# Low parts of the w3 chunks: an accumulating transfer onto a negative copy, in place of a VectorE subtraction

## The chip, the cores and the metric

The kernel runs on one core of one Trainium2 chip. The metric is the time of one execution on the device, in microseconds. The engines are called TensorE (PE), VectorE (DVE), ScalarE (ACT), GpSimd (POOL) and SyncE (SP, which issues the loads).

## What is computed

Two layers of a diffusion backbone over 256 latent tokens and 256 context tokens, in float32. Each layer is a half-step SwiGLU feed-forward sublayer (FFN), a mixer with three branches (mLSTM, a Fourier branch, a convolution), and a second FFN; each sublayer is modulated by a conditioning vector and closed by a layer norm. The change touches only the FFN:

```python
def swiglu(u, w1, w3, w2):
    return (jax.nn.silu(u @ w1) * (u @ w3)) @ w2

def ffn_sublayer(h, mod, w1, w3, w2, g, b):
    u = h * (1 + mod[1]) + mod[0]
    return layer_norm(ALPHA * h + 0.5 * mod[2] * swiglu(u, w1, w3, w2), g, b)

for l in range(DEPTH):
    x = ffn_sublayer(x, ada_x[0], ffn_w1[l, 0], ffn_w3[l, 0], ffn_w2[l, 0], ln_g[l, 0], ln_b[l, 0])
    ...
    x = ffn_sublayer(x, ada_x[2], ffn_w1[l, 1], ffn_w3[l, 1], ffn_w2[l, 1], ln_g[l, 2], ln_b[l, 2])
```

Model width is 1024 and the FFN's inner width 2816, that is 22 blocks of 128. The context runs through the same FFNs except the last.

## The kernel before, in words

Activations lie with their channels on the partitions and the tokens along the free axis: T = 512 columns where latents and context run together, T = 256 in the last FFN. Every float32 product is made from three products of fp32r operands. Both sides are split into a high part, the value rounded to fp32r, and a low part, what is left of it; `mm3` multiplies high by high (line 203), high weight by low activation (line 204) and low weight by high activation (line 205), eight times over the 1024 input channels, so one weight chunk serves 24 matmuls. `split_into` (lines 194 and 195) splits an activation into `opH` and `opL`.

Weights are streamed. `wchunk` (line 178) loads one chunk of 128x1024 float32, 512 KB, into a `raw` buffer by SP (line 186), has ScalarE write the high part `whi` (line 189) and VectorE subtract it from `raw` to the low part `wlo` (line 190). There are four raw buffers (`NR = 4`), and they are shared with `ada_job` (line 219), a background job that computes conditioning columns from `w_ada`: its loads `araw` take the same buffers, and VectorE frees them by its products (lines 236 and 238). High and low parts have five buffers each (`NW = 5`). SP issues loads in program order, and a load waits at the head of SP's queue until its buffer is free.

`gated(fts)` in `ffn` (line 445) takes blocks of the inner width: for each block `ft` it asks for a chunk of w1 and one of w3, multiplies both with the operand into the PSUM tiles `ffps`, and forms silu(first) x second. A w1 chunk and a w3 chunk so alternate. The first two w3 chunks of ffn(0, 0) and their w1 chunks are prepared ahead and kept in `ready`; every other chunk comes from line 453. The chunk work has a raised priority (`PRE = 140` places), by which the scheduler draws it forward in each engine's order. The first call takes two blocks at once and works on column halves where `ready` is empty, that is at the starts of ffn(0, 1) and ffn(1, 0); there its matmuls mix in TensorE's order with those of the sublayer before, whose `closing` (line 410) ends with a layer norm. In that norm GpSimd computes `lnrr` (line 320), a power of a 128x2 tile, once for each of the two token groups, and TensorE spreads it by `lnb` (line 332).

The sequence is ffn(0, 0), mixer(0), ffn(0, 1), ffn(1, 0), mixer(1), ffn(1, 1): about 20 to 420 us, 421 to 1159, 1159 to 1541, 1541 to 1930, 1930 to 2380 and 2381 to 2584 of the span. The last FFN has T = 256; the others have T = 512.

Of the kernel before, what the change touches and what calls it, by code (L numbers as in the profile page):

```python
# [8 lines left out]
F32 = mybir.dt.float32  # L9
F32R = mybir.dt.float32r  # L10
AF = mybir.ActivationFunctionType
ALU = mybir.AluOpType
# [3 lines left out]
P = 128  # L16
# [35 lines left out]
def hybrid_kernel(tc, x, ctx, pos, cc, wada, pcol, w1, w3, w2a, w2b, wst, wv, wg, wbr, wout, dfc, dft, idn, lnrow, out):  # L52
    nc = tc.nc
    es = ExitStack()
    cst = es.enter_context(tc.tile_pool(name="cst", bufs=1))
    wp = es.enter_context(tc.tile_pool(name="wp", bufs=4))
# [8 lines left out]
    def nm(s):  # L65
        cnt[0] += 1
        return f"{s}_{cnt[0]}"

    def slot(name, w=512, dt=F32):
        return sp.tile([P, 516], dt, tag="S", bufs=NS, name=nm(name))[:, :w]  # L70

    def pair(name, T):

        if T <= 256:
            t = slot(name, 512, F32R)
            return t[:, 0:T], t[:, 256:256 + T]
        return slot(name + "H", T, F32R), slot(name + "L", T, F32R)

    def aslot(name, w=512, dt=F32):
        return sp.tile([P, 516], dt, tag="A", bufs=NA, name=nm(name))[:, :w]  # L80
# [13 lines left out]
    def bank(pool, name):  # L94
        return pool.tile([P, 512], F32, tag="ps", name=nm(name))

    act = nc.scalar.activation
# [59 lines left out]
    def bg(n):  # L157
        if busy[0]:
            return
        busy[0] = True  # L160
        while n > 0 and queue:
            try:
                next(queue[0])
                n -= 1
            except StopIteration:
                queue.pop(0)
        busy[0] = False

    def flush():
        while queue:  # L170
            bg(1)
# [4 lines left out]
    def tick():  # L176
        debt[0] += rate[0]
        n = int(debt[0])
        debt[0] -= n
        bg(n)  # L180

    def wchunk(src, w=1024):
        tick()
        with tc.high_priority(offset=PRE):
            raw = wp.tile([P, 1024], F32, tag="raw", bufs=NR, name=nm("raw"))[:, :w]
            nc.sync.dma_start(out=raw, in_=src)
            hi = wp.tile([P, 1024], F32R, tag="hi", bufs=NW, name=nm("whi"))[:, :w]
            lo = wp.tile([P, 1024], F32R, tag="lo", bufs=NW, name=nm("wlo"))[:, :w]
            act(hi, raw, AF.Copy)  # L189
            V.tensor_tensor(lo, raw, hi.bitcast(F32), op=ALU.subtract)  # L190
        return hi, lo

    def split_into(h, l, src):
        act(h, src, AF.Copy)  # L194
        V.tensor_tensor(l, src, h.bitcast(F32), op=ALU.subtract)

    def mm3(ps, W, X, ks, cs, first=True, last=True):
        n = len(ks)
        for i, kt in enumerate(ks):
            wh = W[0][:, i * P:(i + 1) * P]  # L200
            wl = W[1][:, i * P:(i + 1) * P]
            xh, xl = X[kt][0][:, cs], X[kt][1][:, cs]
            PE.matmul(ps, wh, xh, start=first and i == 0, stop=False)  # L203
            PE.matmul(ps, wh, xl, start=False, stop=False)  # L204
            PE.matmul(ps, wl, xh, start=False, stop=last and i == n - 1)  # L205

    def proj(tiles, X, nk, T, halves):

        parts = [XR, CR] if halves and T == 512 else [slice(0, T)]
        for r in parts:  # L210
            for ps, W, *x_only in tiles:
                if r == XR or not any(x_only):
                    mm3(ps[:, r], W, X, range(nk), r)

    def streams(T):
        return [(0, XR)] if T == TX else [(0, XR), (1, CR)]
# [147 lines left out]
    def run_later():  # L364
        while later:
            later.pop(0)()
# [39 lines left out]
    def residual(ps, ys, dt, l, sub, s, r, psr):  # L406
        V.scalar_tensor_tensor(ys[dt][:, r], ps[:, psr], gatecol(l, sub, s, dt), ys[dt][:, r],
                               op0=ALU.mult, op1=ALU.add)

    def closing(ys, l, sub, T, get_chunk, X, ks, nxt):  # L410


        N = Norm()
        O = Output() if nxt is None else None
        tail = TAIL if T == 512 else 0
        U = None
        for dt in range(KT - tail):
            ps = bank(mmp, "clo")
            mm3(ps[:, 0:T], get_chunk(dt), X, ks, slice(0, T))
            for s, r in streams(T):  # L420
                residual(ps, ys, dt, l, sub, s, r, r)
                N.add(s, ys[dt][:, r], T == TX and dt == KT - 1)
            if O and dt:
                O.add(dt - 1, ys[dt - 1], col(l, C_LNG + 8 * sub + dt - 1))
        bcs = {}
        if tail:
            W = {dt: get_chunk(dt) for dt in range(KT - tail, KT)}
            for s, r in streams(T):
                for dt in range(KT - tail, KT):
                    ps = bank(mmp, "clo")  # L430
                    mm3(ps[:, 0:256], W[dt], X, ks, r)
                    residual(ps, ys, dt, l, sub, s, r, slice(0, 256))
                    N.add(s, ys[dt][:, r], s == 0 and dt == KT - 1)
                bcs[s] = N.stats(s)
        if O:
            O.add(KT - 1, ys[KT - 1], col(l, C_LNG + 8 * sub + KT - 1))
            O.finish(N)
            return None
        U = new_operand(T)
        for s, r in streams(T):  # L440
            ln_close(bcs[s] if s in bcs else N.stats(s), s, r, ys, nxt, U)
        later.append(lambda y=ys: rescale(y, l, sub))
        return U

    def ffn(l, i, X, ys, T, nxt):
        sub = 2 * i
        G = {}

        def gated(fts, halves=False):
            tiles = []  # L450
            for ft in fts:
                for n, w in enumerate((w1, w3)):
                    W = ready[ft][n] if ft in ready else wchunk(w[l, i, ft])
                    tiles.append((bank(mmp, "ffps"), W))
                ready.pop(ft, None)
            proj(tiles, X, KT, T, halves)
            for n, ft in enumerate(fts):
                p1, p3 = tiles[2 * n][0], tiles[2 * n + 1][0]
                sg = aslot("sg", T)
                act(sg, p1[:, 0:T], AF.Silu)  # L460
                V.tensor_tensor(sg, p3[:, 0:T], sg, op=ALU.mult)  # L461
                G[ft] = pair("g", T) if T == TX else (aslot("gh", T, F32R), slot("gl", T, F32R))
                split_into(G[ft][0], G[ft][1], sg)

        gated([0, 1], not ready)
        run_later()
        for ft in range(2, 7):
            gated([ft])
        for gi, grp in enumerate(GROUPS):
            def chunk(dt):  # L470
                if gi == 0:
                    return wchunk(w2a[l, i, dt], 768)
                return wchunk(w2b[l, i, gi - 1, dt])
            if gi == 2:
                flush()
                U = closing(ys, l, sub, T, chunk, G, list(grp), nxt)
                break
            for dt in range(KT):
                ps = bank(mmp, "w2ps")
                mm3(ps[:, 0:T], chunk(dt), G, list(grp), slice(0, T))  # L480
                for s, r in streams(T):
                    residual(ps, ys, dt, l, sub, s, r, r)
            for ft in grp:
                del G[ft]
            for ft in range(grp[-1] + 2, min(grp[-1] + 10, FT)):
                gated([ft])
        return U
# [443 lines left out]
    ready = {}  # L931
    for part in range(4):
# [4 lines left out]
        for kt in range(0, KT, 2):  # L937
            raw = wp.tile([P, 1024], F32, tag="raw", bufs=NR, name=nm("araw"))
            for k in range(2):
                nc.sync.dma_start(out=raw[:, 512 * k:512 * k + 512].rearrange("p (v c) -> p v c", v=2),  # L940
                                  in_=wada[0, (kt + k) * P:(kt + k + 1) * P, 0:2 * D]
# [60 lines left out]
NR = 4  # L1002
NW = 5

PRE = 140
# [123 lines left out]
```

## Time and profile before

| what | value |
|---|---|
| median of 3 runs | 2585.43 us (2583.88 to 2587.95) |
| the profiled execution | 2586.51 us |
| its span in the profile | 2584.8 us |
| mean granted clock of TensorE in it | 0.994 |
| bytes moved by queue 1 (all loads and stores of SP) | 351.54 MB |
| w1 and w3 chunks loaded | 176 of 512 KB |

The page of the profile gives busy times of each engine and groups of instructions by source line; the trace behind it gives single instructions with start and length. A releaser in brackets names what ended the idle time before an instruction. `x2` at the end of a row of SP joins two issues, and its length runs from the first to the end of the last. A matmul's length overlaps the next one's: the distance of two starts is what one takes of TensorE. The profiled execution is 1.08 us above the median.

### The profile page before, as it was taken

Reading aid. Unit: us, or ns where it says so; the run is one execution under the profiler, and the core shown is the slowest. Engines: PE = TensorE matmul, PEld = TensorE weight load, DVE = VectorE, ACT = ScalarE, POOL = GpSimd, SP = SyncE. Lnnn points to the kernel's source line nnn. Section 1 sums busy time; section 2 is a strip of 40 time slices with the busy share of each in tenths; the row PEclk is TensorE's granted clock in tenths of the full one; section 3 lists DMA queues with packets and bytes.
Section 4 is the critical chain, followed back from the end, with each engine's and each line's share of the span. In section 5 each row is a group of like instructions: output and inputs, shape, how many; then the busy total and the mean of one; then the engine's idle time right before and its main releaser. Section 6 shows DMA issues by size and latency. Waiting matters only on the chain.

```text
span 2584.8 us, 36771 instructions
## 1 busy us (share of the span) xinstructions
PE 2534.4 (98%) x14354; PEld 2156.9 (83%) x14354; DVE 1789.7 (69%) x3227; ACT 961.9 (37%) x1554; POOL 48.8 (2%) x123
## 2 busy tenths in 40 slices
PE   7999999999999999999999999999999999999998
PEld 4777779788878888888778788877788889999998
DVE  4796776988877765367655467645568888976655
ACT  4222235333432334245222234222235445455543
POOL 0000000010100000000000000000000000000000
PEclk9999999999999999999999999999999999999999
DMA  8565653222223223335544325545523335465663
GB/s 272 177 214 171 184 166 108 88 79 88 64 92 100 78 86 123 91 113 157 162 140 144 124 73 164 177 140 158 158 90 98 119 108 156 151 201 160 188 188 123
DMA packets 130030, 353.89 MB, mean 137 GB/s; under 512 B 12736, under 2 KB 27328, under 8 KB 129856
## 3 DMA queue, kind: packets, MB, share of 16 engines
q1 hardware_dynamic: 129856, 351.54, 43.9%
q8 instruction: 113, 1.85, 0.3%
q14 instruction: 61, 0.50, 0.1%
HBM read 344.12 MB, written 7.34 MB: 136 GB/s over the span
## 4 chain that ended last, share of the span: by engine, by line
PE 86%; DVE 9%; DMA 2%; issue 2%; ACT 1%; POOL 1%; SPq 0%; DVEq 0%; POOLq 0%; ACTq 0%
PE ffps L203 11%; PE ffps L205 11%; PE ffps L204 11%; PE w2ps L203 4%; PE w2ps L204 4%; PE w2ps L205 4%; PE clo L203 3%; PE clo L204 3%; PE clo L205 3%; PE br L203 2%; PE br L204 2%; PE br L205 2%; PE mg L203 2%; PE mg L205 2%; PE mg L204 2%; DVE wlo L190 2%
## 5 line engine op out<-in xcount | busy, mean ns | idle before, releaser
L189 ACT ACTIVATE whi<-raw 128x1024 fp32r<-128x1024 f32 (+1 forms) x498 | 520.5, 1047 | 1199.5 <-issue 272.3
L190 DVE TENSOR_TENSOR wlo<-raw,whi 128x1024 fp32r<-128x1024 f32 (+1 forms) x498 | 599.9, 1206 | 342.5 <-ACT whi L189 337.0
L203 PE MATMUL ffps<-opH,whi 128*128 128x512 f32 (+1 forms) x1120 | 427.7, 385 | 1.8 <-ACT opH L194 1.7
L205 PE MATMUL ffps<-opH,wlo 128*128 128x512 f32 (+1 forms) x1120 | 428.2, 384 | 0.2 <-DVE wlo L190 0.2
L204 PE MATMUL ffps<-opL,whi 128*128 128x512 f32 (+1 forms) x1120 | 426.8, 383 | 0.0
L499 DVE SCALAR_TENSOR_TENSOR cy<-cz,dww,cy 128x482 f32<-128x482 f32 (+29 forms) x480 | 289.0, 602 | 18.1 <-ACT cy L587 11.1
L238 DVE SCALAR_TENSOR_TENSOR acc<-araw,sc,acc 128x512 f32<-128x512 f32 x392 | 273.8, 747 | 27.9 <-DMA araw<-in_wada_dram 26.9
L203 PEld LDWEIGHTS ffps<-opH,whi 128*128 128x128 f32 x1120 | 209.4, 188 | 50.2 <-issue 5.5
L205 PEld LDWEIGHTS ffps<-opH,wlo 128*128 128x128 f32 x1120 | 210.2, 188 | 44.9 <-issue 1.8
L204 PEld LDWEIGHTS ffps<-opL,whi 128*128 128x128 f32 x1120 | 210.4, 188 | 44.2 <-issue 1.2
L461 DVE TENSOR_TENSOR sg<-ffps,sg 128x512 f32<-128x512 f32 (+1 forms) x88 | 54.7, 623 | 116.1 <-PE ffps L205 116.0
L203 PE MATMUL w2ps<-gh,whi 128*128 128x512 f32 x336 | 133.3, 397 | 0.0
L204 PE MATMUL w2ps<-gl,whi 128*128 128x512 f32 x336 | 132.8, 395 | 0.0
L205 PE MATMUL w2ps<-gh,wlo 128*128 128x512 f32 x336 | 132.7, 395 | 0.0
L203 PE MATMUL mg<-opH,whi 128*128 128x512 f32 (+1 forms) x384 | 130.0, 339 | 0.0
L205 PE MATMUL mg<-opH,wlo 128*128 128x512 f32 (+1 forms) x384 | 130.0, 339 | 0.0
L204 PE MATMUL mg<-opL,whi 128*128 128x512 f32 (+1 forms) x384 | 129.8, 338 | 0.0
L203 PE MATMUL qk<-opH,whi 128*128 128x512 f32 (+1 forms) x296 | 102.8, 348 | 0.0
L203 PE MATMUL ffps<-op,whi 128*128 128x256 f32 x352 | 98.9, 285 | 3.2 <-ACT op L194 3.2
L204 PE MATMUL qk<-opL,whi 128*128 128x512 f32 (+1 forms) x296 | 101.7, 344 | 0.0
L205 PE MATMUL qk<-opH,wlo 128*128 128x512 f32 (+1 forms) x296 | 101.4, 343 | 0.0
L204 PE MATMUL ffps<-op,whi 128*128 128x256 f32 x352 | 99.6, 285 | 0.0
(309 smaller groups left out, 5264.8 us busy)
## 6 DMA issues: line engine op xcount, KB each, us to landing
raw<-in_w_dram SPq DMA_DIRECT2D x176, 512.0 KB, 3.6
raw<-in_wst_dram SPq DMA_DIRECT2D x144, 512.0 KB, 3.5
araw<-in_wada_dram SPq DMA_DIRECT2D x128, 512.0 KB, 4.0
raw<-in_w2b_dram SPq DMA_DIRECT2D x64, 512.0 KB, 3.6
raw<-in_wbr_dram SPq DMA_DIRECT2D x48, 512.0 KB, 3.6
raw<-in_w2a_dram SPq DMA_DIRECT2D x32, 384.0 KB, 3.3
araw<-in_wada_dram SPq DMA_DIRECT2D x32, 256.0 KB, 4.9
raw<-in_wv_dram SPq DMA_DIRECT2D x16, 512.0 KB, 3.6
```

The costliest lines, as they stand in the source:

```text
L189: act(hi, raw, AF.Copy)
L190: V.tensor_tensor(lo, raw, hi.bitcast(F32), op=ALU.subtract)
L203: PE.matmul(ps, wh, xh, start=first and i == 0, stop=False)
L204: PE.matmul(ps, wh, xl, start=False, stop=False)
L205: PE.matmul(ps, wl, xh, start=False, stop=last and i == n - 1)
L238: V.scalar_tensor_tensor(accs[s], w, c, accs[s], op0=ALU.mult, op1=ALU.add)
L461: V.tensor_tensor(sg, p3[:, 0:T], sg, op=ALU.mult)
L499: V.scalar_tensor_tensor(dv[:, :, a:b], sv[:, :, a + o:b + o], wcols[:, j:j + 1], dv[:, :, a:b], op0=ALU.mult, op1=ALU.add)
```

## The change

A second chunk function, `wchunk_dma`, stands beside `wchunk`. It loads `raw` as before (its load is line 198 of the changed kernel, its high part line 201), has ScalarE write the negative of the high part into the low part's buffer (line 202), and lets GpSimd issue a transfer of `raw` onto that buffer that adds instead of overwriting (line 203). The low part is then raw minus high, as before. `gated` uses it for w3 wherever `ready` has no chunk: 20 chunks in ffn(0, 0) and 22 in each of the other three FFNs, 86 in all. `mm3` and the loads of w1 and w2 are untouched; the lines behind move down by 13.

```diff
+    def wchunk_dma(src):
+
+        tick()
+        with tc.high_priority(offset=PRE):
+            raw = wp.tile([P, 1024], F32, tag="raw", bufs=NR, name=nm("raw"))
+            nc.sync.dma_start(out=raw, in_=src)
+            hi = wp.tile([P, 1024], F32R, tag="hi", bufs=NW, name=nm("whi"))
+            lo = wp.tile([P, 1024], F32R, tag="lo", bufs=NW, name=nm("wlo"))
+            act(hi, raw, AF.Copy)
+            act(lo, hi.bitcast(F32), AF.Copy, scale=-1.0)
+            nc.gpsimd.dma_start(out=lo.bitcast(F32), in_=raw, accum_op=ALU.add)
+        return hi, lo
...
-                    W = ready[ft][n] if ft in ready else wchunk(w[l, i, ft])
+                    W = ready[ft][n] if ft in ready else (wchunk_dma if n else wchunk)(w[l, i, ft])
```

The program has 86 instructions fewer on VectorE, 86 more on ScalarE and 86 more on GpSimd; SP and TensorE keep their numbers. Three places show how the order moves. They all lie at the start of ffn(0, 1), where `raw_1556` is the chunk of w3[0], `raw_1561` of w1[1] and `raw_1565` of w3[1]; `whi` and `wlo` of each have the next numbers.

ScalarE at the closing of mixer(0), first before: `sq` belongs to the norm, `lnbc` is its result copied out of PSUM.

```order
644 L303 ACTIVATE sq_1493_9285<-y_1448_8997 128x256
645 L293 ACTIVATE sq_1495_9315<-y_1451_9003 128x256
646 L189 ACTIVATE whi_1557_9616<-raw_1556_9614 128x1024
647 L303 ACTIVATE sq_1503_9367<-y_1442_8985 128x256
648 L334 ACTIVATE lnbc_1501_9339<-lnb_1500_9334 128x512
```

And in the change, the same place:

```order
664 L316 ACTIVATE sq_1493_9305<-y_1448_9017 128x256
665 L306 ACTIVATE sq_1495_9335<-y_1451_9023 128x256
666 L201 ACTIVATE whi_1557_9636<-raw_1556_9634 128x1024
667 L316 ACTIVATE sq_1503_9387<-y_1442_9005 128x256
668 L202 ACTIVATE wlo_1558_9637<-whi_1557_9636 128x1024
669 L347 ACTIVATE lnbc_1501_9359<-lnb_1500_9354 128x512
```

The negative copy comes right behind the high part, with one `sq` between them, and ahead of `lnbc`.

GpSimd over the same closing, first before: it had only the powers of the norms here.

```order
66 L320 TENSOR_TENSOR lnrr_1305_8179<-lnred_1304_8176,mhalf_86 128x2
67 L320 TENSOR_TENSOR lnrr_1311_8199<-lnred_1310_8196,mhalf_86 128x2
68 L320 TENSOR_TENSOR lnrr_1499_9331<-lnred_1498_9328,mhalf_86 128x2
69 L320 TENSOR_TENSOR lnrr_1513_9471<-lnred_1512_9468,mhalf_86 128x2
70 L320 TENSOR_TENSOR lnrr_1973_12348<-lnred_1972_12345,mhalf_86 128x2
```

And in the change, the same place:

```order
86 L333 TENSOR_TENSOR lnrr_1305_8199<-lnred_1304_8196,mhalf_86 128x2
87 L333 TENSOR_TENSOR lnrr_1311_8219<-lnred_1310_8216,mhalf_86 128x2
88 L333 TENSOR_TENSOR lnrr_1499_9351<-lnred_1498_9348,mhalf_86 128x2
89 L203 DMA wlo_1558_9637<-raw_1556_9634 128x1024
90 L333 TENSOR_TENSOR lnrr_1513_9491<-lnred_1512_9488,mhalf_86 128x2
91 L203 DMA wlo_1567_9658<-raw_1565_9655 128x1024
92 L203 DMA wlo_1585_9908<-raw_1583_9905 128x1024
```

The transfer of w3[0] stands between the two powers of that closing, and that of w3[1] right behind the second.

TensorE where w3[1] is first read (`ffps_1568` is its product), first before:

```order
5093 L203 MATMUL ffps_1568_9640<-opH_1516_9481,whi_1566_9636 128x256
5094 L204 MATMUL ffps_1568_9640<-opL_1517_9482,whi_1566_9636 128x256
5095 L203 MATMUL ffps_1554_9607<-opH_1524_9489,whi_1552_9603 128x256
5096 L203 MATMUL ffps_1559_9620<-opH_1524_9489,whi_1557_9616 128x256
5097 L203 MATMUL ffps_1564_9633<-opH_1524_9489,whi_1562_9629 128x256
5098 L205 MATMUL ffps_1568_9640<-opH_1516_9481,wlo_1567_9637 128x256
5099 L203 MATMUL ffps_1568_9640<-opH_1518_9483,whi_1566_9636 128x256
```

And in the change, the same place:

```order
5142 L217 MATMUL ffps_1559_9641<-opL_1519_9504,whi_1557_9636 128x256
5143 L216 MATMUL ffps_1554_9627<-opH_1520_9505,whi_1552_9623 128x256
5144 L218 MATMUL ffps_1559_9641<-opH_1518_9503,wlo_1558_9637 128x256
5145 L218 MATMUL ffps_1568_9662<-opH_1516_9501,wlo_1567_9658 128x256
5146 L216 MATMUL ffps_1568_9662<-opH_1518_9503,whi_1566_9657 128x256
5147 L217 MATMUL ffps_1568_9662<-opL_1519_9504,whi_1566_9657 128x256
```

The low part `wlo_1567` is first read at row 5145 instead of row 5098: 47 matmuls of the other three chunks now stand ahead of it. At the start of ffn(1, 0) the same row moves from 6910 to 6957.

## Rows read from the trace of the kernel before

**Rows 1.** The page, part 1: busy us (share of the span) xinstructions
```profile
PE 2534.4 (98%) x14354; PEld 2156.9 (83%) x14354; DVE 1789.7 (69%) x3227; ACT 961.9 (37%) x1554; POOL 48.8 (2%) x123
```

**Rows 2.** Busy time by window: window, length, PE, PEld, DVE, ACT, POOL, clock, DMA share, GB/s
```profile
20.00:100.00 80.00, 76.96 (x467) 52.57 (x467) 54.18 (x110) 36.03 (x65) 0.00 (x0) 1.00 0.75 239
...
1165.00:1528.00 363.00, 363.00 (x1804) 296.38 (x1803) 221.84 (x353) 111.65 (x161) 0.00 (x0) 1.00 0.45 139
1560.00:1910.00 350.00, 349.24 (x1647) 280.40 (x1646) 191.59 (x285) 99.62 (x136) 0.00 (x0) 1.00 0.50 155
2381.00:2550.00 169.00, 168.46 (x1401) 168.46 (x1402) 99.87 (x137) 83.33 (x126) 0.00 (x0) 0.98 0.57 177
```

**Rows 3.** Groups by line and shape: count | busy us, mean ns | idle before, releaser
```profile
L190 DVE TENSOR_TENSOR wlo<-raw,whi 128x1024 fp32r<-128x1024 f32 x466 | 569.3, 1223 | 324.6 <-ACT whi L189 319.1
L189 ACT ACTIVATE whi<-raw 128x1024 fp32r<-128x1024 f32 x466 | 493.4, 1060 | 1101.9 <-issue 247.4 <-PE ffps L204 143.2 <-DMA raw<-in_w_dram 127.8
...
L205 PE MATMUL ffps<-opH,wlo 128*128 128x512 f32 x992 | 393.6, 397 | 0.2 <-DVE wlo L190 0.2
```

**Rows 4.** Timeline, start of ffn(0, 1): start us, length us, engine, line, operation
```profile
1149.53 1.06 ACT L189 ACTIVATE whi<-raw 128x1024 fp32r<-128x1024 f32 x1 [3.53 <-PE clo L204]
...
1151.97 1.22 DVE L190 TENSOR_TENSOR wlo<-raw,whi 128x1024 fp32r<-128x1024 f32 x1
...
1153.25 6.48 SPq L186 DMA_DIRECT2D raw<-in_w_dram  x2
...
1158.16 1.21 DVE L190 TENSOR_TENSOR wlo<-raw,whi 128x1024 fp32r<-128x1024 f32 x1
...
1163.63 0.71 POOL L320 TENSOR_TENSOR lnrr<-lnred,mhalf 128x2 f32<-128x2 f32 x1 [13.11 <-DVE lnred L318]
...
1163.93 1.04 ACT L189 ACTIVATE whi<-raw 128x1024 fp32r<-128x1024 f32 x1
...
1165.80 1.22 DVE L190 TENSOR_TENSOR wlo<-raw,whi 128x1024 fp32r<-128x1024 f32 x1
...
1167.07 0.39 PE L205 MATMUL ffps<-opH,wlo 128*128 128x256 f32 x1
```

**Rows 5.** Timeline of ffn(0, 0), the first w3 chunk made in the stream
```profile
55.97 1.06 ACT L189 ACTIVATE whi<-raw 128x1024 fp32r<-128x1024 f32 x1 [0.91 <-PE ffps L204]
...
57.11 1.22 DVE L190 TENSOR_TENSOR wlo<-raw,whi 128x1024 fp32r<-128x1024 f32 x1
...
63.66 0.39 PE L204 MATMUL ffps<-opL,whi 128*128 128x512 f32 x1
...
63.89 0.39 PE L205 MATMUL ffps<-opH,wlo 128*128 128x512 f32 x1
```

**Rows 6.** Transfers: queue with share of 16 engines; issues with KB, us to landing
```profile
q1 hardware_dynamic: 129856, 351.54, 43.9%
...
raw<-in_w_dram SPq DMA_DIRECT2D x176, 512.0 KB, 3.6
...
cn<-cs SPq DMA_DIRECT2D x8, 256.0 KB, 5.1
...
op<-mid SPq DMA_DIRECT2D x8, 1.0 KB, 1.7
```

**Rows 7.** Timeline, start of ffn(1, 0)
```profile
1547.97 1.22 DVE L190 TENSOR_TENSOR wlo<-raw,whi 128x1024 fp32r<-128x1024 f32 x1
...
1549.25 0.39 PE L205 MATMUL ffps<-opH,wlo 128*128 128x256 f32 x1
```

**Rows 8.** Timeline of ffn(1, 1): one w3 chunk, high part and first reading of its low part
```profile
2472.29 1.06 ACT L189 ACTIVATE whi<-raw 128x1024 fp32r<-128x1024 f32 x1 [1.48 <-issue]
...
2483.78 0.28 PE L205 MATMUL ffps<-op,wlo 128*128 128x256 f32 x1
```

## The prediction

> **What bounds the kernel now.** First I read the busy shares [rows 1]: TensorE is busy 98% of the span, VectorE 69%, ScalarE 37%. So VectorE time that is saved is worth only what TensorE waits for VectorE. Next the same by stage [rows 2]: in stretches of the four FFNs TensorE is busy 76.96 of 80, 363.00 of 363, 349.24 of 350 and 168.46 of 169 us. All its idle time there is 3.04 + 0.76 + 0.54 = 4.34 us, which caps what a lighter VectorE can give in them. Then the groups by line [rows 3]: one low part of 128x1024 costs VectorE 1223 ns, one high part costs ScalarE 1060 ns, and the 992 matmuls that read a low part over 512 columns waited for it 0.2 us in all. The subtraction that goes is nearly free today, because its results stand ready before they are read; what counts is how much later the new ones come.
>
> **The change, part by part.** 86 of the 88 w3 chunks move (two are made ahead and keep the subtraction). VectorE loses 86 x 1.223 = 105 us, all beside TensorE's work. ScalarE gains 86 negative copies of the same shape as the high part, 86 x 1.06 = 91 us, which takes it from 37% to about 41%; its idle time covers that. If it did not, the next operand of TensorE would be late, by 1.06 us. SP's loads keep their number and order. GpSimd gains 86 transfers, each of which waits for its negative copy at the head of GpSimd's queue. At two closings one stands ahead of the second lnrr, which TensorE needs: but that negative copy ends near 1152 and the lnrr starts at 1163.63 [rows 4], so this costs nothing unless one issue takes over 11 us.
>
> The term that decides is the delay **D**, from the end of the negative copy to the landing of the accumulation. The low part is now ready 1.06 + D after the high part; with the subtraction it was 1.3 (57.11 + 1.22 against 55.97 + 1.06 in [rows 5]). A raw buffer is held as much longer, and SP, which waits for a free one, issues the next load later. No accumulating transfer and none issued by GpSimd is in this trace, so D is bounded by [rows 6]. From below: a 1 KB copy lands in 1.7 us. A plain load of 512 KB takes 3.6 us, about 1.9 us above the small one. The accumulation writes 512 KB but reads two sources of that size; at the pace of the load that is 1.7 + 2 x 1.9 = 5.5 us. Issue by GpSimd, nothing at the least and about 0.7 us by its lnrr row [rows 4], brings it to some 6. From above: 256 KB (cn) has a median of 5.1 us, with 1.9 us more for twice the bytes that is 7, and beside loads I let it go to 8. **I take D = 6**, nearest to the load row with a second read, and keep 2 to 8 for the range.
>
> Where is D seen? *Start of ffn(0,1) and of ffn(1,0).* There ada loads hold three raw buffers, and w3[0], w1[1] and w3[1] go one after another through the fourth. Before [rows 4]: w3[0]'s high part starts at 1149.53, its low part ends at 1151.97 + 1.22 = 1153.19 and the next load is issued at 1153.25; that load's low part ends at 1158.16 + 1.21 = 1159.37, and the next issue follows (the same row, two issues, ends at 1153.25 + 6.48 = 1159.73); w3[1]'s high part starts at 1163.93, its low part ends at 1167.02, and TensorE reads it at 1167.07: no reserve at all. After: the negative copy ends at 1149.53 + 2 x 1.06 = 1151.7; w1[1]'s load is issued at 1151.7 + D; its low part is ready 6.1 later (1159.37 − 1153.25), at 1157.8 + D; w3[1]'s high part starts 4.5 after that (1163.93 − 1159.4) and its negative is there 2.1 later; so its low part is ready at 1164.4 + 2D. In the new order TensorE reads it 47 instructions later (row 5145, not 5098). A matmul of 512 columns starts 0.23 us after the one before ([rows 5], 63.66 and 63.89), so one of 256 takes about 0.116, and 47 take 5.5 us: the reading is due at 1172.5. The stall is 2D − 8.1, from D = 4 on: 3.9 us at D = 6. The start of ffn(1,0) shows the same pattern, with a low part that ends at 1547.97 + 1.22 = 1549.19 and is read at 1549.25 [rows 7]. Two starts: **+8 us**.
>
> *ffn(0,0).* The first chunk of this kind has its high part done at 57.03 and its low part read at 63.89 [rows 5]: 6.86 us against 1.06 + 6 = 7.06, 0.2 us short. Behind it each of 20 chunks holds its buffer 5.8 us longer, a quarter of that for each of the four buffers, against a gated tile that takes TensorE 48 x 0.23 = 11 us; the reserve grows more slowly. I put **+2.5 us** at D = 6 and, as the shortfall of 2 us at D = 8 returns in the first few tiles, 8 to 15 there.
>
> *ffn(1,1).* At 256 columns a chunk takes 24 x 0.116 = 2.8 us. From the high part's end at 2472.29 + 1.06 = 2473.35 to the first reading of the low part at 2483.78 are 10.4 us [rows 8], so 1.06 + 6 fits with 3.3 us left. The transfer engines are at 0.57 there [rows 2]. All traffic of queue 1, 351.54 MB, took 43.9% of 16 engines [rows 6] over 2584.8 us, which is 1.69 us of all engines for a load of 512 KB. Two loads and one accumulation with two reads are 4 x 1.69 = 6.8 us against 5.6 us of TensorE for the same two chunks if the second read is charged in full, and 5.1 us if it is not. Only 22 chunks meet this and loads run ahead: **+1 us**, up to 20 at worst (22 x (6.8 − 5.6) = 26 less the reserve).
>
> *Relief of VectorE.* At most the 4.34 us above; I take **−1 us**.
>
> Sum: 8 + 2.5 + 1 − 1 = +10.5 us. The profiled execution took 2586.51 us (span 2584.8 plus 1.71), 1.08 above the median of the three runs: 2597 by its own time, **2596** by the median.
>
> **The rivals.**
> *Hidden.* With D at 4 or less the term 2D − 8.1 is zero, the first chunk's 6.86 us suffice, and the time stays at 2583 to 2588. For it: the load row is 3.6 us with other traffic beside it. Against it: a second source is read, and GpSimd issues. The Trainium skill, page "Collectives: The Full Stack", section "The bandwidth ceiling: the fold count and why AG ≠ RS ≠ AR", says that an add inside a transfer reads two sources and so runs at half rate; by its 31 GB/s for one engine, two reads of 512 KB on 16 engines are an estimated 2.1 us, which gives D near 4 and a sum near zero. No row here shows such an add.
> *Transfers become the bound.* At D = 8 the two starts give 16 us, ffn(0,0) 8 to 15 and ffn(1,1) 5 to 20: 2585 + 29 to 51, so 2614 to 2636, and more beyond. For it: engines 0.75 and 0.57 busy in two of these stages [rows 2]. Against: no compact transfer in [rows 6] is above 5.1 us.
> *GpSimd waits for VectorE.* If GpSimd cannot prepare its transfer while a long VectorE row runs, an issue waits up to the 1.2 us of such a row and D is about 7: the two starts give 12 us, ffn(0,0) 5, ffn(1,1) 2, relief −1, +18 in all, 2603. For it: VectorE is busy 55 to 68% of these stages [rows 2]. Against: GpSimd's lnrr takes 0.71 us beside a busy VectorE [rows 4]. The Trainium skill, page "SBUF — State Buffer", section "Who interferes with whom", states such a lock between VectorE's two-port operations and GpSimd; no run here shows it on a transfer.
> *Faster.* The 105 us matter: ada products, whose VectorE work releases raw buffers, come earlier, the idle time of ffn(0,0) goes (3.04 us of the first 80), and the closings, where VectorE normalises, shorten. It decides from a D under 3.6 on, where the accumulation is no longer than a load. Price: up to −4.3 us in the FFNs and as much in the closings, 2577 to 2581.
>
> **How the numbers follow.** 0.2% (5.2 us) is about what a measurement of this kernel can tell from no change. Likeliest, D between 4.5 and 7: 0.38, of it 0.02 within 0.2%; hidden 0.27; transfers bound 0.18; GpSimd waits 0.10; faster 0.07. So faster 0.07, within 0.2% 0.29, slower 0.64. The range leaves out most of the faster case and the far part of the bound one: 2582 to 2636.
>
> **What would show it.** Right: VectorE near 1685 us, ScalarE near 1053; 86 accumulations that land 5 to 7 us after their issue; TensorE waits for a w3 low part at two places, about 4 us each near 1172 and 1556, and hardly elsewhere. Wrong: no such waits (D under 4), or waits at every w3 chunk of ffn(1,1) with transfer engines near 0.9, or a GpSimd queue that delays the lnrr.

## The result and the profile after

The changed kernel takes 2629.53 us (median of 4 runs, 2627.59 to 2634.86), against 2585.27 us for the kernel before on the same chip: a ratio of 1.0172, 95% interval 1.0161 to 1.0184, or 44 us slower. The forecast had been 2596 us, 11 us slower: the right sign, inside the range, and a loss of a quarter of what came. The profiled execution has a span of 2626.3 us, 41.5 us longer than before.

The page of the profile after, its busy shares [rows 1] and its queues (packets, MB, share of 16 engines; q0 is the queue of the accumulations):

```profile
PE 2545.9 (97%) x14354; PEld 2163.7 (82%) x14354; DVE 1689.1 (64%) x3141; ACT 1044.5 (40%) x1640; POOL 123.8 (5%) x209
...
q1 hardware_dynamic: 129856, 351.54, 42.5%
q0 software_dynamic: 12384, 45.09, 9.4%
...
L203 POOL DMA_DIRECT2D wlo<-raw x86 | 74.6, 868 | 1179.2 <-ACT wlo L202 826.0
...
raw<-in_w_dram SPq DMA_DIRECT2D x176, 512.0 KB, 4.3
...
wlo<-raw POOLq DMA_DIRECT2D x86, 512.0 KB, 5.7
```

VectorE is 100.6 us lighter and ScalarE 82.6 us heavier, near the 105 and 91 of the forecast. An accumulation lands 5.7 us after its issue (median), and GpSimd spends 868 ns on an issue. A load of w1 or w3 now takes 4.3 us where it took 3.6 [rows 6]. TensorE is busy 11.5 us longer although it does the same work, and idle 30 us longer (2626.3 − 2545.9 against 2584.8 − 2534.4).

What TensorE waited for (the waits of PE: us in total, times, longest):

```profile
PE adat L261 <- ACT adar L259: 23.3, 7, 6.3
PE ffps L218 <- DMA wlo<-raw: 7.5, 7, 2.6
```

In the kernel before, the first of these was a single wait of 1.6 us and the second did not exist. `adat` is TensorE's transpose of the `ada` rows, `adar` the ScalarE copy of them out of PSUM. The largest of the seven waits, in the timelines of PE, ACT, SP and POOL:

```profile
96.90 0.39 PE L218 MATMUL ffps<-opH,wlo 128*128 128x512 f32 x1
103.56 0.48 PE L261 MATMUL adat<-ident,adar 128*128 128x128 f32 x1 [6.28 <-ACT adar L259]
...
100.83 1.06 ACT L201 ACTIVATE whi<-raw 128x1024 fp32r<-128x1024 f32 x1 [7.13 <-DMA raw<-in_w_dram]
101.79 0.61 ACT L207 ACTIVATE gh<-sg 128x512 fp32r<-128x512 f32 x1
102.31 1.04 ACT L202 ACTIVATE wlo<-whi 128x1024 fp32r<-128x1024 f32 x1
103.25 0.26 ACT L259 ACTIVATE adar<-adaps 128x128 f32<-128x128 f32 x1
...
88.27 0.38 SPq L241 DMA_DIRECT2D araw<-in_wada_dram  x1
97.21 0.33 SPq L198 DMA_DIRECT2D raw<-in_w_dram  x1
...
88.50 0.86 POOL L203 DMA_DIRECT2D wlo<-raw  x1 [5.48 <-ACT wlo L202]
```

What SP waited for between 88 and 98 us, a single long wait:

```profile
SPq L198 <- DMA wlo<-raw: 8.5, 1, 8.5
```

Read from the POOL row upwards: an accumulation is issued at 88.50, beside a weight load and two ada loads that SP had issued just before, and lands after 8.7 us. SP issues nothing from 88.27 to 97.21, because the next load (the chunk of w3 that comes next) is for the raw buffer that this accumulation reads. So that w3 chunk comes late, ScalarE waits 7.13 us for it, and `adar`, which has long been possible, stands behind its high part and its negative in ScalarE's order. TensorE stands still for 6.28 us at a transpose that has nothing to do with w3. SP as a whole waited 433 us at accumulations (the waits of SP in the kernel after):

```profile
SPq L186 <- DMA wlo<-raw: 234.0, 43, 19.4
SPq L241 <- DMA wlo<-raw: 104.0, 23, 10.2
SPq L198 <- DMA wlo<-raw: 94.8, 19, 10.3
```

Such a wait is not a loss by itself, for SP runs ahead. In the kernel before it waited 1491.9 us at the subtractions:

```profile
SPq L186 <- DVE wlo L190: 1284.3, 329, 20.2
SPq L228 <- DVE wlo L190: 207.6, 76, 6.5
```

It becomes a loss where the load that is held back is needed before it lands, as above.

Behind this wait TensorE also runs slower for a while (busy time by window, columns as in [rows 2]):

```profile
97.00:103.50 6.50, 0.29 (x2) 0.00 (x0) 1.08 (x3) 2.67 (x4) 0.00 (x0) 0.69 0.51 161
103.50:105.00 1.50, 1.44 (x4) 1.25 (x5) 1.50 (x5) 0.01 (x1) 0.86 (x1) 0.50 0.41 29
105.00:107.00 2.00, 2.00 (x7) 1.57 (x7) 2.00 (x5) 0.00 (x0) 0.00 (x0) 0.68 0.82 214
107.00:109.00 2.00, 2.00 (x10) 1.59 (x10) 0.98 (x2) 1.04 (x2) 0.00 (x0) 1.00 1.06 211
```

The granted clock is 0.50 after the wait (the lower of the two levels, 1.2 GHz) and 1.00 again from 107 on. That fits the 11.5 us of extra busy time: TensorE does the same 14354 matmuls at a mean granted clock of 0.989 instead of 0.994.

**Where the time went.** Two matmuls that occur in every kernel serve as marks: the first `pS` of mixer(0) that waits, behind ffn(0,0), and a `br` in mixer(1), behind ffn(0,1) and ffn(1,0). Before, and then after:

```profile
697.52 0.67 PE L648 MATMUL pS<-qk,qk 128*128 128x256 f32 x2 [1.16 <-DVE qk L499]
2162.69 0.39 PE L204 MATMUL br<-op,whi 128*128 128x256 f32 x1 [1.15 <-DVE op L195]
```

```profile
723.60 0.67 PE L661 MATMUL pS<-qk,qk 128*128 128x256 f32 x2 [1.19 <-DVE qk L512]
2199.66 0.39 PE L217 MATMUL br<-op,whi 128*128 128x256 f32 x1 [1.17 <-DVE op L208]
```

26.1 us are lost by the first mark, 10.9 between the marks, and 4.5 from the second to the end of the span. For each run the same three differences against the kernel before, in us, with its median time and its ratio to runs of the kernel before on the same chip. The differences come from one profiled execution of each; the executions of one kernel lie up to 10 us apart (e9: 2598.6 to 2608.4), so a few us between two rows say little.

| run | to mark 1 (ffn(0,0)) | mark 1 to 2 (ffn(0,1), ffn(1,0)) | mark 2 to end (ffn(1,1)) | median us | ratio (95%) |
|---|---|---|---|---|---|
| the change | 26.1 | 10.9 | 4.5 | 2629.5 | 1.0172 (1.0161 to 1.0184) |
| e1 adar on VectorE | 29.2 | 5.1 | 4.4 | 2625.1 | 1.0150 (1.0135 to 1.0165) |
| e2 five raw, four hi/lo | 32.5 | 10.7 | 13.9 | 2640.9 | 1.0215 (1.0199 to 1.0230) |
| e8 the same, kernel before | 7.0 | 4.9 | 0.6 | 2599.4 | 1.0055 (1.0038 to 1.0071) |
| e3 VectorE adds | 1.8 | 1.5 | 0.5 | 2590.1 | 1.0014 (1.0005 to 1.0024) |
| e4 source in memory | 21.6 | 1.0 | 7.2 | 2613.7 | 1.0104 (1.0087 to 1.0121) |
| e5 hold, four copies | 32.0 | 15.0 | 53.4 | 2683.4 | 1.0376 (1.0359 to 1.0394) |
| e9 hold, two copies | 15.1 | −1.3 | 0.7 | 2601.2 | 1.0067 (1.0052 to 1.0083) |
| e6 traffic | 29.5 | 1.2 | 4.2 | 2622.9 | 1.0145 (1.0130 to 1.0160) |
| e10 half the traffic | 14.0 | 1.2 | 0.3 | 2598.9 | 1.0052 (1.0035 to 1.0069) |
| e11 plain copy | 3.9 | 2.8 | 0.9 | 2594.1 | 1.0034 (1.0021 to 1.0047) |
| e12 hold and traffic | 45.5 | 18.5 | 37.3 | 2682.7 | 1.0380 (1.0364 to 1.0395) |
| e7 not in ffn(0,0) | 4.3 | 6.3 | 3.2 | 2601.9 | 1.0061 (1.0046 to 1.0076) |
| e13 VectorE's load back | 36.8 | 10.6 | 4.6 | 2638.1 | 1.0204 (1.0187 to 1.0221) |

Mark 1 in the five runs on which the account of ffn(0,0) rests, e3, e9, e6, e12 and e13 in this order:

```profile
699.34 0.67 PE L661 MATMUL pS<-qk,qk 128*128 128x256 f32 x2 [1.16 <-DVE qk L512]
712.61 0.67 PE L665 MATMUL pS<-qk,qk 128*128 128x256 f32 x2 [1.16 <-DVE qk L516]
727.01 0.67 PE L664 MATMUL pS<-qk,qk 128*128 128x256 f32 x2 [1.16 <-DVE qk L515]
743.01 0.67 PE L664 MATMUL pS<-qk,qk 128*128 128x256 f32 x2 [1.14 <-DVE qk L515]
734.30 0.67 PE L665 MATMUL pS<-qk,qk 128*128 128x256 f32 x2 [1.17 <-DVE qk L516]
```

### The profile page after: what moved, and what is told of

It reads as the page before. It is cut to its first block, busy times and chain, and to the rows that moved or that the text cites. A ratio compares the mean times of both kernels' runs of the same rounds, so it can differ in the third digit from the quotient of the medians.

```text
span 2626.3 us, 36984 instructions
## 1 busy us (share of the span) xinstructions
PE 2545.9 (97%) x14354; PEld 2163.7 (82%) x14354; DVE 1689.1 (64%) x3141; ACT 1044.5 (40%) x1640; POOL 123.8 (5%) x209
## 3 DMA queue, kind: packets, MB, share of 16 engines
q1 hardware_dynamic: 129856, 351.54, 42.5%
q0 software_dynamic: 12384, 45.09, 9.4%
## 4 chain that ended last, share of the span: by engine, by line
PE 69%; DMA 11%; DVE 10%; issue 5%; ACT 3%; POOL 1%; SPq 0%; POOLq 0%; DVEq 0%; ACTq 0%
PE ffps L216 7%; PE ffps L218 7%; PE ffps L217 7%; DMA raw<-in_w_dram 6%; DMA wlo<-raw 4%; DVE wlo L190 3%; PE w2ps L216 2%; PE w2ps L217 2%; PE w2ps L218 2%; PE clo L216 2%; PE clo L217 2%; PE clo L218 2%; DVE cy L512 2%; PE br L217 2%; PE br L216 2%
## 5 line engine op out<-in xcount | busy, mean ns | idle before, releaser
L189 ACT ACTIVATE whi<-raw 128x1024 fp32r<-128x1024 f32 (+1 forms) x412 | 429.6, 1044 | 936.6 <-PE ffps L217 128.4
L190 DVE TENSOR_TENSOR wlo<-raw,whi 128x1024 fp32r<-128x1024 f32 (+1 forms) x412 | 494.9, 1202 | 303.9 <-ACT whi L189 300.0
L201 ACT ACTIVATE whi<-raw 128x1024 fp32r<-128x1024 f32 x86 | 91.1, 1059 | 236.0 <-DMA raw<-in_w_dram 114.9
L203 POOL DMA_DIRECT2D wlo<-raw x86 | 74.6, 868 | 1179.2 <-ACT wlo L202 826.0
L218 PE MATMUL ffps<-op,wlo 128*128 128x256 f32 x352 | 100.1, 286 | 2.9 <-DMA wlo<-raw 2.9
L216 PE MATMUL ffps<-op,whi 128*128 128x256 f32 x352 | 99.5, 287 | 3.3 <-ACT op L207 3.3
```

Source lines behind the costliest of these rows:

```text
L203: nc.gpsimd.dma_start(out=lo.bitcast(F32), in_=raw, accum_op=ALU.add)
```

## The experiments

**First theory: the queue.** The trace after suggests that the loss is `adar` behind a late chunk in ScalarE's order (theory Q), against late low parts (L), shared transfer engines (C) and ScalarE's extra copies (S). Four runs were made on it. All diffs are against the changed kernel unless another is named.

*e1: adar on VectorE.*

```diff
-            act(rows, ps[:, 0:P], AF.Copy)
+            V.tensor_copy(rows, ps[:, 0:P])
```

> The changed kernel, with one edit: the copy of the ada rows out of PSUM (adar) is made by VectorE instead of ScalarE. Theory Q (queue): the accumulation holds a raw buffer some 5 us longer, SP issues the next load late, ScalarE's high part of that chunk waits for it, and adar stands behind that high part in ScalarE's order, so TensorE's transpose adat waits 23 us in seven places and runs at half clock for some us after each. Then adat's waits fall from 23.3 us to under 6, and the time from 2629.5 to about 2598 to 2608. Theory L (late low parts): TensorE waits for the accumulated low parts themselves; then nothing changes, 2625 to 2632. Theory C (transfer engines full): the loads stay late, the wait moves to another tile, 2620 to 2632.

Measured: 2625.1 us, some 4 us better, and none of it in ffn(0,0). That is far from theory Q's 2598 to 2608, and inside what both L and C gave. The waits went elsewhere, as the timeline of PE shows:

```profile
225.05 0.47 PE L261 MATMUL adat<-ident,adar 128*128 128x128 f32 x1 [5.25 <-DVE adar L259]
342.36 0.80 PE L218 MATMUL ffps<-opH,wlo 128*128 128x512 f32 x1 [5.38 <-DMA wlo<-raw]
393.48 0.71 PE L218 MATMUL ffps<-opH,wlo 128*128 128x512 f32 x1 [2.82 <-DMA wlo<-raw]
```

So ScalarE's order is where the lateness surfaces first, not where it comes from: with that way closed, the same chunks are late at VectorE, or at the low part itself. Theory Q falls, as far as it put the cause into ScalarE's order.

*e2: five raw buffers and four pairs of high and low parts.*

```diff
-NR = 4
-NW = 5
+NR = 5
+NW = 4
```

> The changed kernel with five raw buffers instead of four, and four buffers of high and low parts instead of five (there is no more memory). Theory Q: a fifth buffer gives SP the lead back that the longer hold took; adat's waits go to under 8 us, 2590 to 2605 (a little of it lost again by the fourth pair of high and low buffers). Theory L: later landing counts for the same, and four pairs give it less lead: 2630 or more. Theory C: loads are slow because the engines are shared; one buffer more changes little, 2615 to 2630.

Measured: 2640.9 us, in the range of theory L. The control e8, the kernel before with the same numbers, lost 7.0 us to mark 1, so 25.5 of e2's 32.5 belong to the change there, as many as with four buffers (26.1), if the two losses simply add.

> The kernel before with five raw buffers and four buffers of high and low parts: the control for the run of the changed kernel with the same numbers (2641). If the fourth pair is what cost there, ffn(1,0) loses some 20 us here too, 2600 to 2610, and the fifth raw buffer bought ffn(0,0) nothing in the changed kernel. If this stays at 2583 to 2590, the loss belongs to the accumulations with less lead.

Measured for e8: 2599.4 us. Four pairs instead of five have a price of their own (14 us over the whole kernel), and it is spread over the stages. One raw buffer more does not make up for it, and does not repair ffn(0,0); five of both was not tried. In ffn(1,1) e2 lost 13.9 us where e8 lost 0.6 and the change 4.5: with four pairs TensorE waits 10.0 us for low parts there, so late low parts do cost where few buffers hold them.

*e3: the negative copy stays, VectorE adds.*

```diff
-            nc.gpsimd.dma_start(out=lo.bitcast(F32), in_=raw, accum_op=ALU.add)
+            V.tensor_tensor(lo, raw, lo.bitcast(F32), op=ALU.add)
```

> ScalarE still makes the negative copy of all 86 chunks, but VectorE adds raw to it instead of the transfer, so no accumulating transfer is left. Theory Q: the raw buffer is held only 1.06 us longer than in the kernel before; 2586 to 2592. Rival S (ScalarE's 91 us of negative copies delay what stands behind them on ScalarE): 2605 or more, with adat's waits above 10 us.

Measured: 2590.1 us. ScalarE's 86 copies and the slightly longer hold cost 1.4 in a thousand, 4 us; rival S falls. e3 is the base for the runs that follow.

*e4: the accumulation reads w3 again from memory.* The low part is also written as fp32r here instead of as float32.

```diff
-            nc.gpsimd.dma_start(out=lo.bitcast(F32), in_=raw, accum_op=ALU.add)
+            nc.gpsimd.dma_start(out=lo, in_=src, accum_op=ALU.add)
```

> The changed kernel, with the accumulation reading w3 again from memory (HBM) instead of the raw buffer. The raw buffer is free after the high part, earlier than in the kernel before; the low part still lands D after the negative copy, and the engines carry 45 MB more of reads from memory. Theory Q: adat's waits fall under 6 us, and the starts of ffn(0,1) and ffn(1,0) lose their chain through the buffer: 2583 to 2595. Theory C: the same load on the transfer engines, so 2620 or more. Theory L: the low parts are as late as before, 2620 or more.

Measured: 2613.7 us, between the theories. With the raw buffer free early, the stretch of ffn(0,1) and ffn(1,0) lost 1.0 us instead of 10.9: there the loss needs the held buffer. ffn(0,0) still lost 21.6. Something beside the raw buffer costs there: the traffic, or the low parts, which come later than in the change (7.3 us from issue to landing).

**Second theory: hold and traffic.** A transfer by GpSimd does three things: it keeps the raw buffer (theory H), it moves bytes through the engines that bring the loads (theory T), and its result is late. The next runs take them one at a time, on top of e3.

*e5 and e9: hold alone.* VectorE makes the low part; GpSimd copies 8 columns of the raw buffer to a scratch tile, four times (e5) or twice (e9).

```diff
+            V.tensor_tensor(lo, raw, lo.bitcast(F32), op=ALU.add)
+            for _ in range(4):
+                nc.gpsimd.dma_start(out=hs8, in_=raw[:, 0:8])
```

> As in the run with negative copies and a VectorE addition (2590), and in addition each of the 86 raw buffers is kept for some 8 us after its load has landed: GpSimd copies 8 columns of it to a scratch tile four times, one after another. No low part is later, and the transfer engines carry next to nothing more. Theory H (the buffer that is held longer starves the ring of loads in ffn(0,0)): 2605 to 2620, the loss in ffn(0,0). Theory T (the accumulations' own traffic slows the loads beside them, which arrive in bursts there): 2588 to 2596.

Measured: 2683.4 us. Four copies keep a buffer 14.1 us after its load has landed in ffn(0,0) (mean of 20), while the changed kernel keeps it 8.3: too large a dose, and at T = 256 far too large (53.4 us lost there). So two copies:

> The run with buffers held and no traffic, with two small copies instead of four. Four kept a raw buffer 14.1 us in ffn(0,0) after its load had landed, the changed kernel keeps it 8.4 us; two should keep it about 7 us. If the hold alone, at the changed kernel's own length, explains ffn(0,0), that stage loses 12 us or more (total 2605 or more). If it only did so at twice the length, the stage loses under 5 us: 2590 to 2597.

Measured: 2601.2 us; the hold came out at 5.8 us, somewhat shorter than in the changed kernel, and ffn(0,0) lost 15.1 us, 13.3 more than e3. Hold alone does harm there, with next to no traffic (0.72 MB on GpSimd's queue against 45.09). Between the marks it cost nothing at this length (−1.3).

*e6, e10, e11: traffic alone.* VectorE makes the low part; GpSimd accumulates the high part onto a scratch tile in memory, in full (e6), half of its columns (e10), or copies it without adding (e11).

```diff
+            V.tensor_tensor(lo, raw, lo.bitcast(F32), op=ALU.add)
+            nc.gpsimd.dma_start(out=dscr, in_=hi.bitcast(F32), accum_op=ALU.add)
```

> As in the run with negative copies and a VectorE addition (2590), and in addition GpSimd accumulates each of the 86 high parts onto a scratch tile in memory (HBM) that nobody reads: the traffic of 86 accumulations of 512 KB, without a raw buffer held and without a late low part. Theory H: 2588 to 2596. Theory T: 2605 to 2625, the loss in ffn(0,0), where the engines are busiest.

> The run with traffic only, with 512 of the 1024 columns accumulated: half the bytes, 86 transfers. Theory T with a threshold (loads are late only where a burst fills the engines): ffn(0,0) loses 3 to 10 us instead of 27, 2594 to 2602. If each transfer costs by being issued and not by its bytes, the loss stays above 20 us.

> The run with traffic only, with a plain copy of the same 512 KB instead of an accumulation, so one source is read and not two. If the second read is what makes the accumulation heavy, its time on the engines falls from 10.4% of the span toward 6%, it lands about 4 us after issue instead of 6.1, and ffn(0,0) loses 8 to 16 us instead of 27: 2598 to 2608. If not, 2615 to 2625.

Measured: 2622.9, 2598.9 and 2594.1 us. ffn(0,0) lost 27.7, 12.2 and 2.1 us more than e3. The queues and issues of e6 and of e11:

```profile
q0 software_dynamic: 12384, 45.09, 10.4%
...
dscr<-whi POOLq DMA_DIRECT2D x86, 512.0 KB, 6.1
```

```profile
q0 software_dynamic: 12384, 45.09, 4.7%
...
dscr<-whi POOLq DMA_DIRECT2D x86, 512.0 KB, 3.9
```

The same bytes and packets take 2.2 times as long on the engines when they are added, and land 2.2 us later. A plain copy of 512 KB for every w3 chunk nearly fits beside the loads; the addition does not. With half the bytes the loss is nearly half, between the two cases that the expectation named. In these runs the transfer keeps a buffer of the high parts; in e6 ScalarE waited for that three times, 10.3 us in all, each time in ffn(1,1) and never in ffn(0,0).

*e12: hold and traffic, low parts on time.* As e6, but from `raw`.

```diff
+            V.tensor_tensor(lo, raw, lo.bitcast(F32), op=ALU.add)
+            nc.gpsimd.dma_start(out=dscr, in_=raw, accum_op=ALU.add)
```

> Buffers held and traffic together, but no low part late: the accumulation reads raw, as in the changed kernel, and goes to a scratch tile in memory, while VectorE makes the low part by an addition. If hold and traffic are the cause and the late low part is not, ffn(0,0) loses 22 to 32 us, and the starts of ffn(0,1) and ffn(1,0) lose what the chain through one buffer costs there: 2618 to 2632. If the late low parts matter, under 2610.

Measured: 2682.7 us, far more than expected. To mark 1 it lost 43.7 us over e3, about hold plus traffic (13.3 + 27.7 = 41.0), so a low part need not be late at all. The buffer was kept 6.9 us there, less than in the changed kernel. Between the marks hold and traffic together cost 18.5 us, where e9 and e6 alone cost −1.3 and 1.2. The 37.3 us at the end belong at least in part to the scratch tile, which the changed kernel does not have: in ffn(1,1) GpSimd waited 16 times for the transfer before, 118.4 us in all, and the transfers landed in 8.1 us (median), while TensorE takes about 5.6 us for two chunks by the prediction's working. In e6 the same waits (15, 97.2 us) held no raw buffer, and cost 4.2.

*e7: ffn(0,0) left as it was.*

```diff
-(wchunk_dma if n else wchunk)(w[l, i, ft])
+(wchunk_dma if n and (l, i) != (0, 0) else wchunk)(w[l, i, ft])
```

> The changed kernel, but ffn(0,0) keeps the VectorE subtraction: 66 of 86 chunks moved. All theories that put most of the loss into ffn(0,0) expect the loss of that stage, some 25 us, to go: 2600 to 2608. If the stages are not independent (a delay in ffn(0,0) hides one later), 2608 to 2620.

Measured: 2601.9 us. 21.8 of the 26.1 us to mark 1 go, and the other stages do not get worse (6.3 and 3.2 us instead of 10.9 and 4.5); all in all 27.7 us hang on 20 of the 86 chunks.

*e13: VectorE's load put back.* Alone, the two causes add up to 41 us in ffn(0,0), but the changed kernel loses only 24.3 over e3.

```diff
             nc.gpsimd.dma_start(out=lo.bitcast(F32), in_=raw, accum_op=ALU.add)
+            for c in (0, 512):
+                V.tensor_tensor(vs, raw[:, c:c + 512], hi[:, c:c + 512].bitcast(F32), op=ALU.subtract)
```

> The changed kernel, with VectorE's load put back: for each of the 86 chunks VectorE makes the subtraction into a scratch tile that nobody reads (two halves of 512 columns). Buffers, transfers and low parts are as in the changed kernel. Hold alone cost ffn(0,0) 13.5 us and traffic alone 27.3, together 43.0, but the changed kernel loses 24.5 there. If the lighter VectorE is what gives some 16 us back (it frees the ada buffers earlier), ffn(0,0) now loses 35 to 43 us and the time is 2638 to 2655. If the scratch tile in memory made the traffic of those runs dearer than the changed kernel's own, ffn(0,0) stays at 22 to 28 us and the time at 2628 to 2634.

For the four losses that the expectation names the table has 13.3, 27.7, 43.7 (e12) and 24.3 us, all over e3. Measured: 2638.1 us, 36.8 us to mark 1, 10.7 more than the changed kernel (8.6 more by the two median times). The lighter VectorE thus gives back about 10 us there. That it does so by freeing the ada buffers earlier fits SP's waits for VectorE's ada products in this stage (40 to 420 us of the span), 98.8 us in the changed kernel and 111.9 here, but was not tested by itself. The rest of the gap (41 against 35) may be the dearer scratch transfers, 10.4% against 9.4% of the span; that was not separated.

No run beats the kernel before.

## Why the prediction was wrong in size

**Right.** VectorE came to 1689.1 us (about 1685 forecast) and ScalarE to 1044.5 (1053). The deciding quantity was right: D was put at 6 us; the negative copy of the timeline above ends at 102.31 + 1.04 = 103.35, GpSimd issues at 103.64, and the median from issue to landing is 5.7, together 6.0. GpSimd did not wait for VectorE: each of the 86 issues follows the end of its negative copy by 0.3 us (once 1.0) and takes 868 ns, 1031 at most. So the rival "GpSimd waits for VectorE", which named the Trainium skill, page "SBUF — State Buffer", section "Who interferes with whom", shows nothing here. TensorE's waits for `lnrr` also stayed as they were, 6.5 us in 11 times.

**Near in number, only partly for the reason given.** The starts of ffn(0,1) and ffn(1,0) were put at 8 us. Between the marks 10.9 were lost, and 1.0 when the accumulation does not hold the buffer (e4). The chain through the fourth buffer runs as forecast, and TensorE waits for w3[1]'s low part at both starts, but only 1.19 and 1.23 us: D was 4.9 to 5.0 us for w3[0] and w3[1] of both stages, for which 2D − 8.1 is under 2. Of the rest, 6.4 us are waits of `adat` (1.97, 2.64 and 1.79 us), which the prediction did not have, and the second of them lies at 1334.7, far behind the start; behind that one the clock also falls to 0.50. That 8 comes near 10.9 is in part luck.

**The term that failed: ffn(0,0), +2.5 us; it cost 26.1** (24.3 over e3). The step was "each of 20 chunks holds its buffer 5.8 us longer, a quarter of that for each of the four buffers, ...; the reserve grows more slowly". Three things were wrong in it. It weighed the hold against the reserve of the w3 low parts alone, though the buffers are shared with the ada loads, SP issues in order, and any load behind a held buffer is late, whoever needs it. What TensorE waited for was mostly not a low part but `adat`, whose `adar` stands behind a late w3 chunk in ScalarE's order: 16.9 us of `adat` against 2.2 us of low parts in this stage. The hold alone makes 13.3 us (e9, at 5.8 us of hold). It charged the traffic to ffn(1,1) alone. There it cost little; ffn(0,0), where weight and ada loads together fill the engines to 0.61 and 0.63 already, went to 0.68 and 0.76, and its traffic alone makes 27.7 us (e6). The rows of before and of after, by window:

```profile
60.00:160.00 100.00, 98.37 (x488) 76.82 (x487) 82.72 (x134) 26.31 (x37) 0.00 (x0) 1.00 0.61 189
160.00:240.00 80.00, 80.00 (x385) 63.33 (x384) 64.41 (x100) 25.34 (x33) 0.00 (x0) 1.00 0.63 193
```

```profile
60.00:160.00 100.00, 92.39 (x446) 72.58 (x445) 70.47 (x117) 28.87 (x38) 3.45 (x4) 0.97 0.68 197
160.00:240.00 80.00, 74.70 (x362) 57.78 (x360) 50.62 (x85) 27.94 (x35) 6.03 (x7) 0.96 0.76 212
```

A mean of 0.76 hides the bursts: the accumulation issued at 88.50 has three loads beside it and lands after 8.7 us. And no term allowed for the clock: TensorE's busy time grew by 11.5 us over the whole kernel.

**ffn(1,1), +1 us; it cost 4.5**: one wait of 2.58 us for a low part at 2438.10, near the start, where the reserve is short, and half clock after it.

**Relief of VectorE, −1 us.** The cap of 4.34 us was right for the kernel before, where nothing waits for VectorE. Once buffers are short it is worth more, by the account of e13 because VectorE's products free the ada buffers: 10.7 us in ffn(0,0). It is a gain only on a loss that the change itself made.

**The rivals.** "Transfers become the bound" gave 2614 to 2636 and came nearest, but its condition, D = 8, was not met: at D = 6 the engines and buffers of ffn(0,0) were already too short. The upper end of the range came from that rival, so that the time lies inside the range is luck. "Hidden" fell with D. The Trainium skill, page "Collectives: The Full Stack", section "The bandwidth ceiling: the fold count and why AG ≠ RS ≠ AR", has the addition at half rate for its two reads: the ratio is about that here (10.4% against 4.7%, 2.2 times). The estimate of 2.1 us of all engines from its rate was low: 9.4% of 2626.3 us over 86 transfers are 2.9 us.

## What to carry to other kernels

A transfer that takes over an engine's work also takes the buffer it reads and a share of the engines that bring the loads: price both against whatever else uses that ring, not against the reserve of its own result. Look for the stage in which a second stream of loads shares the buffers, and for the in-order queues behind them (SP, then ScalarE, then TensorE): the wait appears at the first instruction that stands behind a late chunk, and moving that instruction away (e1) only moves the wait. Saving time on an engine that nobody waits for is no gain to set against any of this.

## What the runs showed of the hardware

An accumulating transfer of 512 KB between two SBUF tiles lands in 5.7 us (median; 9.7 at most) and takes 2.9 us of all 16 engines, 1.7 times a load of the same size (42.5% of 2626.3 us for 351.54 MB, 1.66 us for 512 KB); a plain copy by GpSimd of the same size, from SBUF to memory, lands in 3.9 (e11). GpSimd is busy 0.87 us with each issue and was not held up by VectorE. The three waits of TensorE for `adat` of 4.7 to 6.3 us were each followed by a granted clock of 0.50 for some 3 to 6 us, so that they cost more than their own length; behind the wait that ended at 325.56 of the kernel after (windows, columns as in [rows 2], and two matmuls):

```profile
327.00:329.00 2.00, 2.00 (x6) 1.52 (x6) 2.00 (x4) 0.00 (x0) 0.00 (x0) 0.50 0.83 221
329.00:332.00 3.00, 3.00 (x10) 2.33 (x9) 3.00 (x6) 0.00 (x0) 0.00 (x0) 0.57 0.64 201
...
327.12 0.63 PE L216 MATMUL ffps<-opH,whi 128*128 128x512 f32 x1
327.55 0.63 PE L217 MATMUL ffps<-opL,whi 128*128 128x512 f32 x1
```

A matmul of 512 columns starts every 0.43 us there, where at full clock one starts every 0.23 us.
